# A hybrid HGRN2 and gMLP block on one core: blocks of w_out split at the border, and TensorE's work at the end of phase one held in written order

## The chip, the cores and the metric

The kernel runs on one core of a Trainium2 chip. A core has five engines with an instruction stream each: TensorE (PE in the profile, its weight loads PEld), VectorE (DVE), ScalarE (ACT), GpSimd (POOL) and SyncE (SP, which here issues the DMAs). Each works through its own stream in order; between engines, semaphores make an instruction wait for data or for a buffer. The metric is the device time of one execution in microseconds (us); lower is better.

## The reference

One layer of a diffusion backbone on 2048 latent tokens with a context prefix of 256 tokens, all in fp32:

```
h   = modulate(rmsnorm(x), shift1, scale1)             # 2048 x 1024
p   = h @ w_in                                         # 1024 -> 5*512 + 2*512 columns
o_f = gated recurrence, forward  (4 heads, 128x128 state, started from the context's state)
o_b = gated recurrence, backward (own forget gate)
o_hg  = rmsnorm(o_f + o_b) * silu(gate)                # per head of 128 channels
o_mlp = gelu(u) * (W_s layernorm(gelu(v)) + b)         # chunks of 128 positions
x   = x + g1 * (concat(o_hg, o_mlp) @ w_out)           # 1024 -> 1024
h2  = modulate(rmsnorm(x), shift2, scale2)
a,g = split(h2 @ w_up)                                 # 2 x 2816 columns
x   = x + g2 * ((a * gelu(depthwise_conv3x3(g) + b)) @ w_down)
out = rmsnorm(x, norm_final)
```

The six modulation vectors come from a product of silu(c) with w_ada.

## The kernel before

**Products.** An fp32 product is done as three passes on TensorE with operands split in two parts: hi is a rounded copy (a cast, by ScalarE, L133) and lo the rest (a subtraction, L134, by VectorE or GpSimd). The passes are hi·hi, hi·lo and lo·hi, so a 128-row block of the inner dimension takes three matmuls of 512 columns. Small products in the recurrence (banks named mi and sc) run on fp32 operands directly; one such 128x128 product is two records in the trace. All matmuls go through `T.matmul`, so their line is always L65, and all transposes are on L69.

**Phases.** Phase 1 (to 974 us) is the w_in projection, for the two halves of the tokens one after the other (hh = 0, 1) and in banks of 24 matmuls (`pj<-xh,whi`, `xl,whi`, `xh,wlo`). Phase 2 is the w_out product (`dn<-wo,o`, 16 tiles of 128 tokens, 48 matmuls each) with the second norm. Phase 3, to about 2007 us, is w_up, with a recursive scheme of fewer products (units ux and uz), and the convolution on VectorE and ScalarE (L1430, L1433). Phase 4 is w_down (`dn<-thl,mhl`), and then the rows' last norm and the stores.

**A head of the recurrence.** `hg` makes, for each head and half, the scores (sc), the products vt,kt that are the chunks' contributions to the states (`mi<-vt,kt`, copied to fs and bs_), and two chains over 8 chunks on VectorE (`chain`): the forward one over fs (L777), and the backward one over bs_ (L783). Then come the output products of a chunk, `mi<-vt,sc` (L895), `mi<-fs,Q` (L896) and in the second half of the tokens `mi<-bs_,Q` (L898). Four chunks make one tile on, which ScalarE copies out (L903) and squares for its norm (L758); GpSimd makes the root (rk, L128), VectorE scales by it (on<-on,rk, L737), TensorE transposes (`mi<-ident,on`), VectorE gates (L767), and a DMA stores the result to oT. The backward part of the first half has to wait for the second half's chain; `deferred` (L922) loads its data again (bs, Qb, op, sgb, L928 to L931), runs the backward chain and the products `mi<-bs,Qb` (L939), and goes the same way.

**Order.** All this is written as generators in two queues, hg_q and bg_q (class Pump). `yield w` means that the next step is due w us later on a clock that adds up estimated times of TensorE's matmuls (`T.t`). `slot()`, called between the matmuls of a projection bank, runs the steps that are due, and `later(fn, w)` adds a single step. So the steps of a head are mixed among pj matmuls. `drain()` runs all remaining steps at once and minds no due time. The instructions written in this way then go through a scheduler which may reorder them on each engine; `pin` (keep_in_program_order) holds an instruction at its written place among the pinned ones of its engine.

**The border from phase 1 to phase 2.** Ahead of the fourth last projection bank a hook calls `open_wo` (L1126):

```
hg_q.drain()
gates_done()
bg_q.drain()
```

Then it opens the pool for w_out's blocks and adds a step that loads the first o tile (L1138), the blocks wo (L1144) and, later, splits o tile 0. The blocks of w_out have been scaled by g1, split into hi and lo and stored to memory in the middle of phase 1 (`split` and `st` at L994 and L995). The raw data of o tile 1 are loaded at the start of phase 2 (L1316, `raw_o`). The last steps of the gMLP part, the products wsT,nt and the evictions nt (L717) with their stores (L686), stand at the very end of phase 1.

Of the kernel before, what the change touches and what calls it, by code (L numbers as in the profile page):

```python
# [32 lines left out]
LV = [1, 2, 4, 8, 16, 32, 64]  # L33
AL = 512


# [17 lines left out]
class Tensor:  # L54


    def __init__(self, engine):
        self.engine, self.t = engine, 0.0

    def matmul(self, out, lhsT, rhs, **kw):  # L60
        n = 1
        for _, count in rhs.ap[1:]:
            n *= count
        self.t += n / 2400 + 0.0135 if rhs.dtype == F32R else 2 * max(0.112, n / 1200 + 0.005)
        return self.engine.matmul(out, lhsT, rhs, **kw)  # L65

    def transpose(self, out, in_, identity):
        self.t += 0.109
        return self.engine.transpose(out, in_, identity)  # L69

# [13 lines left out]
def tile_trunk(ctx, tc, x, c, cx, c_ctx, w_ada, b_ada, norm_mix, norm_ffn, w_in, hg_norm, sgu_g, sgu_b,  # L84
# [14 lines left out]
    make_identity(nc, ident)  # L99
    ones = cst.tile([P, P], F32, name="ones")  # L100
    G.memset(ones, 1.0)
    ones_r = cst.tile([P, P], F32R, name="ones_r")
    nc.gpsimd.tensor_copy(ones_r, ones)
    vec = cst.tile([P, 50], F32, name="vec")
# [86 lines left out]
    with es1:  # L191
# [536 lines left out]
        def gate_later(hh, h, g0, on, r, sg):  # L728
            at = {"key": (hh, h), "to": (hh, h, g0, on, sg), "r": r}
            gates.append(at)  # L730
            hg_q.later(lambda: o_scale(at), 4.0)
            hg_q.later(lambda: gate_now(at), 7.5)

# [57 lines left out]
        def hg(hh, h, F, K, qs, vt, sgt):  # L791
# [90 lines left out]
            else:  # L882
# [3 lines left out]
                st(sg_d[h], sgt)  # L886
            yield 7.0 if hh == 1 else 4.0
            on = []
# [33 lines left out]
        def deferred(h):  # L922

            Qb = ph.tile([P, 2, TH], F32, tag="Q", name="Qb", align_bytes=AL)[:, 0, :]
            sgt = ph.tile([P, NCH + 1, P], F32, tag="fs", name="sgb")[:, :NCH, :].rearrange("p c t -> p (c t)")
            op = ph.tile([P, TH], F32, tag="S", name="op")
            bs_ = ph.tile([P, NCH + 1, P], F32, tag="bst", name="bs2")
            ld(bs_[:, :NCH, :], dh_d[h].rearrange("p (c t) -> p c t", t=P))  # L928
            ld(Qb, qb_d[h])
            ld(op, op_d[h])  # L930
            ld(sgt, sg_d[h])  # L931
            yield 5.0
            chain(bs_, True, hb[h], lambda i: tb0[h][:, i:i + 1])
            yield 4.0
            on = []
            for g in range(0, NCH, 4):
                po = bank("mi")
                for i in range(4):
                    T.matmul(po[:, i * P:(i + 1) * P], Qb[:, (g + i) * P:(g + i + 1) * P], bs_[:, g + i + 1, :],  # L939
                             start=True, stop=True)  # L940
# [41 lines left out]
        def w_out_ops():  # L982

            for n in range(2):
                cl = slice(n * 512, n * 512 + 512)
                g = pm.tile([P, 512], F32, tag="acc", name="g1")
                ld(g, g_d[0:1, cl].broadcast_to([P, 512]))
                for k in range(NK):
                    raw = raw_tile().rearrange("p (a c) -> p a c", a=2)
                    hi, w = raw[:, 0, :], raw[:, 1, :]  # L990
                    ld(w, w_out[k * P:(k + 1) * P, cl])
                    yield 8.0
                    V.tensor_mul(w, w, g)
                    split(hi.bitcast(F32R), w.bitcast(F32R), w, V)  # L994
                    st(wo_d[:, k, :, cl], raw)  # L995
                    yield 1.5
# [130 lines left out]
        def open_wo():  # L1127
# [8 lines left out]
            def load():  # L1136
                raw = raw_tile().rearrange("p (k c) -> p k c", c=P)
                ld(raw, oT_d[0][:, :, 0:P])  # L1138
                for k in range(early, NK):
                    wo.append(pw.tile([P, 2, D], F32R, name=f"wo{k}", align_bytes=AL))  # L1140
# [20 lines left out]
        bg_q.drain()  # L1161
        hg_q.flush()


# [14 lines left out]

    turn = [0]  # L1180

# [3 lines left out]
    def zbank():  # L1185
        return ps2.tile([P, 512], F32, tag="uz", name="uz", bufs=2)

# [4 lines left out]
    def dbank():  # L1192
        return ps2.tile([P, 2, 512], F32, tag="dn", name="dn", bufs=2)

    def a_tiles():
        return tuple(px.tile([P, 4, P], F32R, tag=w, name=w, bufs=4, align_bytes=AL) for w in ("Ah", "Al"))

# [3 lines left out]
    def c_tile():  # L1201
        return px.tile([P, NK, P], F32R, tag="fl", name="fl", bufs=2, align_bytes=AL)

# [4 lines left out]
    class Unit:  # L1208
# [15 lines left out]
        def prep(self, i):  # L1224
# [6 lines left out]
            if i == 1:  # L1231
                self.s2 = (c_tile()[:, :4, :].bitcast(F32) if self.slots[0] == 1 else
                           px.tile([P, 4, P], F32, tag="s1", name="s2"))
            split(hi, lo, (a11, a12, self.s2, a11, a21, a12, a22)[i])
# [38 lines left out]
    with tc.tile_pool(name="po", bufs=1, reuse_waits="tile") as po:  # L1273
        def second_norm(hh, g0, xs, ss, bank_, first, step):
# [6 lines left out]
            for k in range(4):  # L1281
# [14 lines left out]
                V.tensor_sub(fl[:, 6, :], fl[:, 1, :], fl[:, 2, :])  # L1296
                hi = px.tile([P, 7, P], F32R, tag="yst", name="yst", bufs=2, align_bytes=AL)
                a = b = 0
# [20 lines left out]
        def split_o(t, raw):  # L1319
            o = po.tile([P, 2, NK, P], F32R, tag="o", name="o", align_bytes=AL) if t % 2 else first_o[0]()  # L1320
            split(o[:, 0], o[:, 1], raw, V, pin)
# [6 lines left out]

        raw_o = {1: fetch_o(1)}
        xts = {0: fetch_x(0)}  # L1330
        ops = {0: first_o[1]}
        xs = []
# [208 lines left out]
    def cast(n, a, b, at, bt):  # L1541

        split(*at, a, V)
        split(*bt, b, V)
        ops[n] = *at, *bt
# [20 lines left out]
    for n, (u, i) in enumerate(prods):  # L1566
# [20 lines left out]
        if n == 12:  # L1587
            edges = px.tile([P, 7, P], F32R, tag="yst", name="edges", bufs=2, align_bytes=AL).bitcast(F32)
            edges = edges[:, :4, :].rearrange("p f (w c) -> p f w c", w=2)
# [129 lines left out]
    def root(ss, plus=D * EPS):  # L1719

        a, r = (pd_.tile([P, 1], F32, tag=t, name=t, bufs=4) for t in ("ra", "rr"))
        G.tensor_scalar(out=a, in0=ss, scalar1=plus, scalar2=None, op0=ALU.add)  # L1722
        G.tensor_tensor(out=r, in0=a, in1=mhalf[:, :1], op=ALU.pow)  # L1723
# [139 lines left out]
```

## Time and profile before

| | |
|---|---|
| median of 3 runs | 2437.95 us (2434.5 to 2441.58) |
| the profiled execution | 2440.39 us |
| its span, first to last instruction | 2438.6 us |
| mean granted clock of TensorE | 0.996 of full speed |
| TensorE busy | 2402.0 us, 99% |
| VectorE, ScalarE, GpSimd busy | 1656.9, 1043.2, 867.8 us |

The profiled execution is 2.44 us above the median and lies within the runs' scatter. In rows of the timeline the columns are the start, the length, the engine, the line and the operation, output<-inputs, the shape and how many instructions the row holds; in brackets stands how long the engine was idle before the row and what ended that. A row of several instructions runs from the first one's start to the last one's end, and matmuls overlap, so the spacing of many (11.15 us for 48) is the cost of one, not the length of a record. The granted clock is what the throttle allowed TensorE, 1.00 being full speed.

### The profile page before, as it was taken

The numbers are of one execution on the slowest core, as the hardware profiler recorded it, in microseconds if no ns is written. First come the engines' busy times: TensorE is split into PE (matmuls) and PEld (weight loads), VectorE is DVE, ScalarE is ACT, GpSimd is POOL, SyncE is SP. The second block draws the span as 40 slices with busy tenths as digits, with TensorE's granted clock in tenths as the row PEclk, the third lists the DMA queues.
The fourth block names the chain that finished last, engine by engine and source line by source line (L and its number), as shares of the span: only waits on it lengthen the run. The fifth ranks groups of instructions, "written<-read, shape, count | busy, mean of one in ns | idle before, by whom it ended". The sixth has DMA issues, their size and how long they took to land.

```text
span 2438.6 us, 32286 instructions
## 1 busy us (share of the span) xinstructions
PE 2402.0 (99%) x11711; PEld 1995.0 (82%) x11711; DVE 1656.9 (68%) x2253; ACT 1043.2 (43%) x1802; POOL 867.8 (36%) x788
## 2 busy tenths in 40 slices
PE   8999999999999999999999999999999999999998
PEld 5887887888888888788888888888888887888887
DVE  5757795765786785465596666639866772776875
ACT  3654344444444443354554444434445442332343
POOL 0021110210121122000688778787888870000002
PEclk9999999999999999999999999999999999999999
DMA  8365445463355234668922322562222238934755
GB/s 302 117 206 169 148 143 168 153 234 111 114 195 173 88 103 160 223 208 264 303 80 90 96 81 91 179 235 97 86 94 85 88 112 336 324 121 147 229 152 198
DMA packets 305581, 396.43 MB, mean 163 GB/s; under 512 B 32633, under 2 KB 215681, under 8 KB 302349
## 3 DMA queue, kind: packets, MB, share of 16 engines
q1 hardware_dynamic: 302132, 393.61, 48.6%
q8 instruction: 92, 1.51, 0.3%
q10 hardware_dynamic: 3289, 0.76, 0.1%
q14 instruction: 68, 0.56, 0.1%
HBM read 285.18 MB, written 109.13 MB: 162 GB/s over the span
## 4 chain that ended last, share of the span: by engine, by line
PE 54%; issue 2%; DMA 1%; DVE 1%; POOL 1%; ACT 1%; SPq 0%; POOLq 0%; ACTq 0%; DVEq 0%
PE dn L65 20%; PE ux L65 19%; PE uz L65 14%; PE pj L65 0%; POOL ra L1722 0%; DMA raw<-in_x_dram 0%; POOL rr L1723 0%; PE ux L69 0%; DMA raw<-in_w_up_dram 0%; DMA yf<-yd 0%; PE uz L69 0%; DVE dn L1433 0%; DMA yd<-fl 0%; POOL Al L134 0%; DVE cv L1357 0%
## 5 line engine op out<-in xcount | busy, mean ns | idle before, releaser
L1433 DVE SCALAR_TENSOR_TENSOR dn<-gp,taps,dn 128x1024 f32<-128x1024 f32 x352 | 448.2, 1284 | 97.5 <-ACT dn L1430 93.1
L65 PE MATMUL dn<-thl,mhl 128*128 128x512 f32 x1680 | 381.5, 389 | 1.2 <-ACT thl L133 1.2
L65 PEld LDWEIGHTS dn<-thl,mhl 128*128 128x128 f32 x1680 | 315.0, 188 | 67.7 <-ACT thl L133 2.1
L134 POOL TENSOR_TENSOR Al<-raw,Ah 128x512 fp32r<-128x512 f32 x264 | 341.7, 1311 | 65.8 <-ACT Ah L133 41.5
L65 PE MATMUL pj<-xh,whi 128*128 128x512 f32 x896 | 362.3, 405 | 0.3 <-ACT whi L133 0.3
L65 PE MATMUL pj<-xh,wlo 128*128 128x512 f32 x896 | 351.1, 392 | 1.2 <-DVE wlo L134 1.2
L65 PE MATMUL pj<-xl,whi 128*128 128x512 f32 x896 | 351.7, 393 | 0.0
L133 ACT CAST Ah<-raw 128x512 fp32r<-128x512 f32 x264 | 162.9, 620 | 238.9 <-PE ux L65 133.1
L65 PE MATMUL ux<-xah,Ah 128*128 128x512 f32 x528 | 205.7, 390 | 0.3 <-ACT keep L1497 0.3
L65 PEld LDWEIGHTS pj<-xh,wlo 128*128 128x128 f32 x896 | 168.3, 188 | 37.5 <-DVE wlo L134 2.1
L65 PEld LDWEIGHTS pj<-xh,whi 128*128 128x128 f32 x896 | 168.7, 188 | 34.2 <-issue 3.5
L65 PEld LDWEIGHTS pj<-xl,whi 128*128 128x128 f32 x896 | 168.9, 189 | 30.0 <-DVE xl L253 0.2
L65 PE MATMUL dn<-wo,o 128*128 128x512 f32 x768 | 184.4, 396 | 2.6 <-ACT o L133 2.1
L65 PE MATMUL uz<-yf,Ah 128*128 128x512 f32 x704 | 174.0, 389 | 0.0
L65 PEld LDWEIGHTS dn<-wo,o 128*128 128x128 f32 x768 | 143.0, 189 | 32.8 <-ACT o L133 2.5
L591 POOL TENSOR_TENSOR K<-K,tot 128x512 f32<-128x512 f32 x40 | 62.9, 1572 | 299.9 <-DVE tot L521 154.6
L65 PE MATMUL ux<-yf,Ah 128*128 128x512 f32 x528 | 155.4, 389 | 0.0
L65 PEld LDWEIGHTS uz<-yf,Ah 128*128 128x128 f32 x704 | 132.1, 188 | 27.4
L65 PE MATMUL ux<-xah,Al 128*128 128x512 f32 x528 | 141.8, 390 | 1.0 <-POOL Al L134 0.9
L65 PE MATMUL ux<-xal,Ah 128*128 128x512 f32 x352 | 137.0, 389 | 0.0
L1722 POOL TENSOR_SCALAR ra<-ss 128x1 f32<-128x1 f32 x8 | 5.3, 662 | 360.4 <-ACT jk L1714 360.4
L134 DVE TENSOR_TENSOR wlo<-raw,whi 128x1024 fp32r<-128x1024 f32 x68 | 84.1, 1236 | 68.3 <-ACT whi L133 67.3
(341 smaller groups left out, 4452.7 us busy)
## 6 DMA issues: line engine op xcount, KB each, us to landing
raw<-in_w_up_dram SPq DMA_DIRECT2D x88, 512.0 KB, 3.6
mr<-m SPq DMA_DIRECT2D x85, 512.0 KB, 5.5
raw<-in_w_in_dram SPq DMA_DIRECT2D x68, 512.0 KB, 4.0
sT<-wd SPq DMA_DIRECT2D x88, 256.0 KB, 5.8
raw<-in_w_ada_dram SPq DMA_DIRECT2D x32, 512.0 KB, 4.6
yf<-yd SPq DMA_DIRECT2D x14, 1024.0 KB, 10.4
m<-cv SPq DMA_DIRECT2D x22, 544.0 KB, 2.7
raw<-in_w_down_dram SPq DMA_DIRECT2D x22, 512.0 KB, 4.0
```

The lines of the kernel that those rows point to most:

```text
L65: return self.engine.matmul(out, lhsT, rhs, **kw)
L133: keep(S.copy(hi, raw))
L134: (eng or G).tensor_sub(lo, raw, hi.bitcast(F32))
L591: e.tensor_mul(view(K2, row * W + o, src), view(K, o, src), view(tot, t0, [[4, n], [ts, 2], [0, B]]))
L1433: V.scalar_tensor_tensor(out=cr, in0=gt[:, t // 3:t // 3 + RH, t % 3:t % 3 + GW], scalar=taps[:, t * NF + f:t * NF + f + 1], in1=cr, op0=A ...
L1722: G.tensor_scalar(out=a, in0=ss, scalar1=plus, scalar2=None, op0=ALU.add)
```

## The change

It has these parts; the prediction refers to them by number.

1. `LATE`: the w_out blocks 5, 6 and 7 are stored scaled but unsplit, loaded raw into the place of their lo part, and split after phase 1's last step, by six casts on ScalarE and six subtractions on VectorE, all pinned.
2. `T.keep`: class Tensor passes each instruction through a function that is the identity at first. In the last head, `hg` for (1, 3), it becomes `pin` once the states are written, and the identity again after phase 1's last step. In between all of TensorE's matmuls and transposes keep their written order.
3. Wider steps: the waits 7.5, 7.0 and 4.0 become 8.7, 8.5 and 4.8 for the last head's steps.
4. The raw data of o tile 1 are loaded in `open_wo`, into a tile of their own.
5. The tile ones goes; ones_r is made from ident, and the other users read it through a bitcast.
6. Pools of phases 2 and 3: the order of the first banks, one tag for Ah and Al with 8 buffers, two tags for uz, some alignments and a padded tile.
7. Phase 4: odd tiles 0 to 4 are allocated ahead of thl, and the evictions to odd (S.copy) and the casts of operands 3 and later are pinned.
8. The last norm's `root` adds a tensor operand with tensor_add in place of a tensor_scalar with a pointer.

```diff
+LATE = (5, 6, 7)
...
-        self.engine, self.t = engine, 0.0
+        self.engine, self.t, self.keep = engine, 0.0, lambda i: i
...
-        return self.engine.matmul(out, lhsT, rhs, **kw)
+        return self.keep(self.engine.matmul(out, lhsT, rhs, **kw))
...
-        return self.engine.transpose(out, in_, identity)
+        return self.keep(self.engine.transpose(out, in_, identity))
...
-    ones = cst.tile([P, P], F32, name="ones")
-    G.memset(ones, 1.0)
     ones_r = cst.tile([P, P], F32R, name="ones_r")
-    nc.gpsimd.tensor_copy(ones_r, ones)
+    nc.gpsimd.tensor_scalar(out=ones_r, in0=ident, scalar1=0.0, scalar2=1.0, op0=ALU.mult, op1=ALU.add)
+    ones = ones_r.bitcast(F32)
...
-            hg_q.later(lambda: gate_now(at), 7.5)
+            hg_q.later(lambda: gate_now(at), 8.7 if (hh, h) == (0, NH - 1) else 7.5)
...
-            yield 7.0 if hh == 1 else 4.0
+            if (hh, h) == (1, NH - 1):
+                T.keep = pin
+            yield 8.5 if (hh, h) == (1, NH - 1) else 7.0 if hh == 1 else 4.0
...
             chain(bs_, True, hb[h], lambda i: tb0[h][:, i:i + 1])
-            yield 4.0
+            yield 4.8 if h == NH - 1 else 4.0
...
-                    split(hi.bitcast(F32R), w.bitcast(F32R), w, V)
-                    st(wo_d[:, k, :, cl], raw)
+                    if k in LATE:
+                        st(wo_d[:, k, 0, cl], w)
+                    else:
+                        split(hi.bitcast(F32R), w.bitcast(F32R), w, V)
+                        st(wo_d[:, k, :, cl], raw)
...
-                        ld(wo[k][:, :, sl].bitcast(F32), wo_d[:, k, :, sl])
+                        if k in LATE:
+                            ld(wo[k][:, 1, sl].bitcast(F32), wo_d[:, k, 0, sl])
+                        else:
+                            ld(wo[k][:, :, sl].bitcast(F32), wo_d[:, k, :, sl])
+                raw1 = pw.tile([P, NK, P], F32, name="raw1")
+                ld(raw1, oT_d[0][:, :, P:2 * P])
+                first_o.append(raw1)
                 yield 17.0
...
         hg_q.flush()
+        T.keep = lambda i: i
+        for n in range(2):
+            sl = slice(n * 512, n * 512 + 512)
+            for k in LATE:
+                t = wo[k][:, :, sl]
+                split(t[:, 0], t[:, 1], t[:, 1].bitcast(F32), V, pin)
...
-        raw_o = {1: fetch_o(1)}
+        raw_o = {1: first_o[1]}
...
-        split(*at, a, V)
-        split(*bt, b, V)
+        keep = pin if 3 <= n < 6 * NJ else lambda i: i
+        split(*at, a, V, keep)
+        split(*bt, b, V, keep)
...
+    odd = [pd_.tile([P, 2, 512], F32, name=f"odd{i}") for i in range(5)]
     thl = pd_.tile([P, 3, 2, 512], F32R, name="thl", align_bytes=AL)
-    odd = [pd_.tile([P, 2, 512], F32, name=f"odd{i}") for i in range(NCH)]
+    odd += [pd_.tile([P, 2, 512], F32, name=f"odd{i}") for i in range(5, NCH)]
...
-        G.tensor_scalar(out=a, in0=ss, scalar1=plus, scalar2=None, op0=ALU.add)
+        if isinstance(plus, float):
+            G.tensor_scalar(out=a, in0=ss, scalar1=plus, scalar2=None, op0=ALU.add)
+        else:
+            G.tensor_add(a, ss, plus)
...
-            S.copy(o[:, q // 2, :], pd)
+            pin(S.copy(o[:, q // 2, :], pd))
```

What this does to the order of instructions is seen on TensorE at the end of phase 1. Before, the first outputs of the last head stand among projection matmuls; here is TensorE's order from the last states (vt,kt) on:

```order
L65 MATMUL mi<-vt,kt 128x128 x16
...
L65 MATMUL mi<-vt,sc 128x128
L65 MATMUL mi<-fs,Q 128x128
...
L65 MATMUL pj<-xh,whi 128x512
L65 MATMUL pj<-xl,whi 128x512
L65 MATMUL pj<-xh,wlo 128x512
...
L65 MATMUL mi<-bs__7975,Q 128x128
```

From vt,kt to the last transposes of on stand 55 pj matmuls in all, and 41 come behind those. A bit later in the same stream, still before the change, are the products of `deferred` (bs, Qb) and the transposes of on:

```order
L65 MATMUL pj<-xh,whi 128x512
L65 MATMUL pj<-xl,whi 128x512
L65 MATMUL mi<-bs_8079,Qb 128x128 x4
L69 MATMUL mi<-ident,on 128x128 x8
L65 MATMUL pj<-xh,wlo 128x512
L65 MATMUL pj<-xh,whi 128x512
L65 MATMUL mi<-bs_8079,Qb 128x128 x4
L65 MATMUL pj<-xl,whi 128x512
```

Here too pj matmuls stand ahead of the first four products, behind the first eight transposes and behind the second four products. After the change, TensorE has from the same states on:

```order
L66 MATMUL mi<-vt,kt 128x128 x16
L66 MATMUL mi<-vt,sc 128x128
L66 MATMUL mi<-fs,Q 128x128
L66 MATMUL mi<-bs__7961,Q 128x128
...
L66 MATMUL mi<-bs_8065,Qb 128x128 x4
L70 MATMUL mi<-ident,on 128x128 x8
L66 MATMUL mi<-bs_8065,Qb 128x128 x4
L70 MATMUL mi<-ident,on 128x128 x8
L66 MATMUL pj<-xh,whi 128x512
L66 MATMUL pj<-xl,whi 128x512
L66 MATMUL pj<-xh,wlo 128x512
```

No pj matmul is left between the states and the last transposes, and all 96 follow them; the lines of the new file are one higher here. The rows left out hold the other outputs of the head, three products a chunk.

SyncE's queue at the border was, before the change:

```order
L1144 DMA wo_8181<-wo_d 128x2x512
L1144 DMA wo_8182<-wo_d 128x2x512
L1144 DMA wo_8183<-wo_d 128x2x512
L686 DMA oT_80<-nt 128x512 x2
L1316 DMA raw<-oT_79 128x8x128
L1326 DMA raw<-in_x_dram 128x1024
L1316 DMA raw<-oT_79 128x8x128
```

The load of o tile 1's raw data, the first raw<-oT here, stands behind both stores of nt. After the change the queue is:

```order
L1150 DMA wo<-wo_d 128x512 x3
L1152 DMA wo<-wo_d 128x2x512 x2
L1150 DMA wo<-wo_d 128x512 x3
L1154 DMA raw_8180<-oT_77 128x8x128
L686 DMA oT_78<-nt 128x512 x2
L1347 DMA raw<-in_x_dram 128x1024
L1337 DMA raw<-oT_77 128x8x128
```

The load of o tile 1's raw data (raw_8180) has moved ahead of the two stores of nt, and six of the wo loads carry half the data.

More of the change, by code (lines that the diff above doesn't have):

```diff
@@ L1139, in load @@
                 for k in range(early, NK):
-                    wo.append(pw.tile([P, 2, D], F32R, name=f"wo{k}", align_bytes=AL))
+                    wo.append(pw.tile([P, 2, D], F32R, tag="wo", name="wo", bufs=NK - early, align_bytes=AL))
                 for n in range(2):
@@ L1178, in tile_trunk @@
     xal = pb.tile([P, NR - 1, 4, 512], F32R, tag="xal", name="xal", align_bytes=AL)
-    turn = [0]
+    turn = [0, 0]
     def xbank():
@@ L1185, in zbank @@
     def zbank():
-        return ps2.tile([P, 512], F32, tag="uz", name="uz", bufs=2)
+        turn[1] += 1
+        return ps2.tile([P, 512], F32, tag=f"uz{turn[1] % 2}", name="uz")
     def ubank():
@@ L1193, in dbank @@
         return ps2.tile([P, 2, 512], F32, tag="dn", name="dn", bufs=2)
+    for first in (xbank, zbank, dbank, zbank):
+        first()
     def a_tiles():
-        return tuple(px.tile([P, 4, P], F32R, tag=w, name=w, bufs=4, align_bytes=AL) for w in ("Ah", "Al"))
+        return tuple(px.tile([P, 4, P], F32R, tag="A", name=w, bufs=8, align_bytes=AL) for w in ("Ah", "Al"))
     def v_tile():
@@ L1201, in c_tile @@
     def c_tile():
-        return px.tile([P, NK, P], F32R, tag="fl", name="fl", bufs=2, align_bytes=AL)
+        return px.tile([P, NK, P], F32R, tag="fl", name="fl", bufs=2)
     def raw_tile2(j):
@@ L1232, in prep @@
                 self.s2 = (c_tile()[:, :4, :].bitcast(F32) if self.slots[0] == 1 else
-                           px.tile([P, 4, P], F32, tag="s1", name="s2"))
+                           px.tile([P, 4 * P + 80], F32, tag="s1", name="s2")[:, :4 * P].rearrange("p (k c) -> p k c", k=4))
             split(hi, lo, (a11, a12, self.s2, a11, a21, a12, a22)[i])
@@ L1296, in second_norm @@
                 V.tensor_sub(fl[:, 6, :], fl[:, 1, :], fl[:, 2, :])
-                hi = px.tile([P, 7, P], F32R, tag="yst", name="yst", bufs=2, align_bytes=AL)
+                hi = px.tile([P, 7, P], F32R, tag="yst", name="yst", bufs=2)
                 a = b = 0
@@ L1319, in split_o @@
         def split_o(t, raw):
-            o = po.tile([P, 2, NK, P], F32R, tag="o", name="o", align_bytes=AL) if t % 2 else first_o[0]()
+            o = po.tile([P, 2, NK, P], F32R, tag="o", name="o") if t % 2 else first_o[0]()
             split(o[:, 0], o[:, 1], raw, V, pin)
@@ L1327, in fetch_x @@
             return xt.rearrange("p a b -> p (a b)")
-        raw_o = {1: fetch_o(1)}
+        raw_o = {1: first_o[1]}
         xts = {0: fetch_x(0)}
-        ops = {0: first_o[1]}
+        ops = {0: first_o[2]}
         xs = []
@@ L1587, in tile_trunk @@
         if n == 12:
-            edges = px.tile([P, 7, P], F32R, tag="yst", name="edges", bufs=2, align_bytes=AL).bitcast(F32)
+            edges = px.tile([P, 7, P], F32R, tag="yst", name="edges", bufs=2).bitcast(F32)
             edges = edges[:, :4, :].rearrange("p f (w c) -> p f w c", w=2)
```

## The prediction

> **What bounds the kernel now.** I read the busy times of the page first, then its chain of what ended last:
>
> ```profile
> PE 2402.0 (99%) x11711; PEld 1995.0 (82%) x11711; DVE 1656.9 (68%) x2253; ACT 1043.2 (43%) x1802; POOL 867.8 (36%) x788
> PE 54%; issue 2%; DMA 1%; DVE 1%; POOL 1%; ACT 1%; SPq 0%; POOLq 0%; ACTq 0%; DVEq 0%
> ```
>
> TensorE is busy in nearly the whole span of 2438.6 us. So an edit counts if it opens or closes idle time on TensorE, or changes its clock. What can be closed is in TensorE's list of waits:
>
> ```profile
> PE dn L65 <- ACT o L133: 2.1, 1, 2.1
> PE dn L65 <- DVE o L134: 0.5, 1, 0.5
> PE dn L65 <- ACT thl L133: 1.2, 2, 0.8
> PE mi L65 <- DVE bs__7975 L783: 0.6, 1, 0.6
> ```
>
> Columns: total, count, longest. The first two are the stall on o tile 1, the third is phase 4, and the last is the place that edit 2 touches. The timeline shows that place and the border to the w_out product; in 128x128 fp32 rows two records are one product:
>
> ```profile
> 935.64 0.39 PE L65 MATMUL mi<-vt,sc 128*128 128x128 f32 x2
> 936.84 0.49 PE L65 MATMUL mi<-fs,Q 128*128 128x128 f32 x2 [0.37 <-DVE fs L777]
> 939.34 0.46 PE L65 MATMUL mi<-bs__7975,Q 128*128 128x128 f32 x2 [0.63 <-DVE bs__7975 L783]
> 943.80 0.39 PE L65 MATMUL mi<-bs__7975,Q 128*128 128x128 f32 x2
> 951.95 1.13 PE L65 MATMUL mi<-bs,Qb 128*128 128x128 f32 x8 [0.47 <-issue]
> 959.27 0.63 PE L69 MATMUL mi<-ident,on 128*128 128x128 f32 x4 [1.00 <-DVE on L737]
> 961.04 0.65 PE L69 MATMUL mi<-ident,on 128*128 128x128 f32 x4 [0.45 <-DVE on L737]
> 973.57 11.15 PE L65 MATMUL dn<-wo,o 128*128 128x512 f32 x48
> 986.80 0.73 PE L65 MATMUL dn<-wo,o 128*128 128x512 f32 x2 [2.08 <-ACT o L133]
> 988.06 18.24 PE L65 MATMUL dn<-wo,o 128*128 128x512 f32 x73 [0.52 <-DVE o L134]
> ```
>
> Between 936 and 962 TensorE idles only 0.37 + 0.63 + 0.47 + 1.00 + 0.45 = 2.9 us, because projection products (pj) fill the time that VectorE, ScalarE and POOL need for the head's chain of steps.
>
> **Edit 2 and 3, the written order and the wider steps.** In the order of before, 55 pj products stand between the last state product (vt,kt) and the last transposes of on; 41 follow. In the order of after none stands between and all 96 follow: the drain at the border runs the rest of the head at one go, so the wider waits (8.5, 8.7, 4.8) have nothing to act on, and I cost edit 3 at 0. The other engines' orders there are unchanged. So TensorE meets three waits bare. Their ends come from these rows of VectorE, ScalarE and SyncE:
>
> ```profile
> 938.46 2.28 DVE L783 SCALAR_TENSOR_TENSOR bs__7975<-bs__7975,tot 128x128 f32<-128x128 f32 x6
> 945.14 0.56 ACT L903 COPY on<-mi 128x512 f32<-128x512 f32 x1
> 948.56 0.69 DVE L737 TENSOR_TENSOR on<-on,rk 128x512 f32<-128x512 f32 x1 [1.23 <-POOL rk L128]
> 949.17 2.67 DVE L783 SCALAR_TENSOR_TENSOR bs<-bs,tb 128x128 f32<-128x128 f32 x7
> 944.27 0.32 SPq L928 DMA_DIRECT2D bs<-dh  x1
> ```
>
> A: the third product of the written order (bs,Q of chunk 0) needs the last of the backward chain's steps, which end at 938.46 + 2.28 = 940.74. vt,sc and fs,Q of chunk 0 are through at about 936.1 (935.64 and two products). Idle 4.7 us.
> The 22 products left take 22 x 0.23 = 5.1 us (943.80 - 939.34 = 4.46 for about 20), so they end at 945.9, 1.7 later than before (943.80 + 0.39 = 944.2).
> B: now the second half is copied out by ScalarE, normed, scaled (on<-on,rk), and then comes VectorE's second backward chain. Before, the copy began at 945.14, behind the first half's squares, and the chain at 949.17. Now it can begin at about 945.95, 0.8 later, while the reload of the states (bs<-dh), which waits for TensorE's last read, goes out 1.7 later. The chain slips by 0.8 to 1.7; I take 1.0, near the lower end, since the scaling at 948.56 and not the load was last before. The first bs,Qb product comes at about 952.95: idle 7 us.
> C: the gaps from that product to the two transposes of on are the same work, 959.27 - 951.95 = 7.32 and 961.04 - 959.27 = 1.77, so they begin at 960.3 and 962.0, with some 4.0 and 1.3 us idle in front.
> Up to here the head is 1.0 late. But the 55 products still have to be done: 55 x 11.15/48 = 12.7, with the 0.2275 us spacing inside such a run 12.5. Slip at full clock: 12.5 + 1.0 = **+13.5**.
>
> **What the idle time does to the clock.** The windows of 1 us around the stall on o tile 1 (busy time, granted clock, DMA share, GB/s):
>
> ```profile
> 985.00:986.00 1.00, 0.00 (x0) 1.00 1.14 332
> 986.00:987.00 1.00, 0.20 (x1) 1.00 0.84 306
> 987.00:988.00 1.00, 0.53 (x2) 0.81 0.23 84
> 988.00:989.00 1.00, 0.94 (x2) 0.50 0.07 29
> 990.00:991.00 1.00, 1.00 (x4) 0.50 0.68 178
> 991.00:992.00 1.00, 1.00 (x5) 0.98 1.14 382
> 956.00:962.00 6.00, 4.55 (x26) 1.00 0.09 35
> ```
>
> After 2.08 + 0.52 us idle the granted clock was 0.50 from about 987.6 to 991.0, 3.4 us in which half the work was done: 1.7 us lost. The 1.00 + 0.45 us at 957 to 961 cost no clock. A, B and C are each longer than 2.6 us. A dip behind A or C falls on dense products, 1.7 each; behind B only about 2.7 us of products stand before C's wait, so at most 1.1 reaches the path: 1.7 + 1.1 + 1.7 = **+4.5**. Ends: 0 and, with a fourth, 6.8.
> The Trainium skill (TensorE: Matmul & The Clock Gate, Part 1) says that the clock is halved after at least one wholly idle window of about 3.4 us. The trace disagrees: it fell after 2.08 and 0.52 us with work in between. By that rule the sum would hold 1.7 for one dip, behind B, in place of 4.5.
>
> **Edit 4, o tile 1's raw data loaded ahead of the stores.** What held it before, and the late split's neighbours:
>
> ```profile
> 973.43 2.95 SPq L686 DMA_DIRECT2D oT<-nt  x2
> 976.48 0.83 SPq L1316 DMA_DIRECT2D raw<-oT  x1
> 973.85 0.75 DVE L717 SCALAR_TENSOR_TENSOR nt<-mi,vec,rh 128x512 f32<-128x512 f32 x1 [1.59 <-PE mi L65]
> L134 DVE TENSOR_TENSOR raw<-raw x16: 673/688/1767, 376.7 to 537.5; 128x512 fp32r<-128x512 f32 x16
> ```
>
> The load went out at 976.48, behind two stores that waited for the last nt. Moved ahead of them it depends only on the o stores of phase 1's first half, which stand earlier in SyncE's queue; the two stores now stand behind it and keep their own wait for the last nt. The 2.08 + 0.52 and the dip go: **-2.6 - 1.7 = -4.3**.
>
> **Edit 1, three w_out blocks split at the border.** Six casts and six of the 16 subtractions of the last row (its figures: least, median, most ns) leave the time from 376 to 537 us. No wait of TensorE there that I found ends on them: 0. They come back behind the last nt, which VectorE ends at 974.60, 1.03 after the product's start. At 0.69 each, block 5's first half is ready 1.7 after that start; its products are the 16th and later, due at 15 x 0.2275 = 3.4. The others follow with more room, and o tile 1 is due only after 11.15. Cost 0, with a cover of 1.7; if all six had to be through first, 6 x 0.69 + 1.03 - 3.4 = 1.8, with a dip 3.5. The loads are half as large; nothing waits for them.
>
> **Edits 5 to 8.** Rows for phase 4, the tail and the start:
>
> ```profile
> 2027.75 12.58 PE L65 MATMUL dn<-thl,mhl 128*128 128x512 f32 x54 [0.75 <-ACT thl L133]
> 2072.07 8.25 PE L65 MATMUL dn<-thl,mhl 128*128 128x512 f32 x35 [0.46 <-ACT thl L133]
> 2433.04 0.50 POOL L1722 TENSOR_SCALAR ra<-oss 128x1 f32<-128x1 f32 x1 [1.56 <-ACT dn L1748]
> 14.89 0.19 POOL L126 TENSOR_SCALAR rs<-xss 128x2 f32<-128x2 f32 x1 [12.31 <-ACT xjk L239]
> 1.45 4.42 PE L65 MATMUL pj<-ident 128*128 128x128 f32 x24 [1.45 <-POOL ident masks.py:199]
> 1.63 0.95 POOL L269 MEMSET acc<- 128x1024 f32 x1
> 6.98 3.59 PE L65 MATMUL pj<-wa,cs 128*2 128x512 f32 x8 [1.10 <-DMA wa<-in_w_ada_dram]
> ```
>
> Casts of thl no longer stand behind evictions (pinned in written order): at best both waits go, -1.2; at worst 0, as the pins only reorder ScalarE. I take **-1.2**. The last root's add gets a tensor operand in place of a pointer: 0.50 could fall to the 0.19 of an add with constants, or stay; **-0.3**, of the 0.0 to -0.3 that one link of the tail allows. At the start ident comes some 0.85 later, behind the 0.95 memset and with the one of ones gone: the 4.42 us of warming products end at 6.7 in place of 5.9, and the first real ones wait for data until 6.98: 0, with 0.3 of cover. Pools and paddings of phases 2 and 3 move no instruction: 0.
>
> **Sum.** 13.5 + 4.5 - 4.3 - 1.2 - 0.3 = +12.2 us, against the profiled execution (2440.39 us, 2.4 above the median). On the median of 2437.95 that gives **2450 us**.
>
> **Rivals.**
> The clock falls only when TensorE idles through one whole stretch of 3.4 us, the length of the dip at 987.6. Such stretches laid end to end, only B's 7 us is certain to hold one: 13.5 + 1.7 - 5.8 = +9.4, 2447.3 us. Against it stands that this dip came without such a stretch. Chance 0.12. This is the rule of the Trainium skill named above (TensorE: Matmul & The Clock Gate, Part 1).
> No clock loss at all, as at 957 to 961: 13.5 - 5.8 = +7.7, 2445.6. These stretches are three times as long. 0.07.
> The other side: the border is covered. If TensorE's waits A to C held projection products after all, since the steps are due later, the slip would be 0 and the gains alone remain, -5.8: 2432 us. It decides once the slip falls under 5.8, which needs 34 of the 55 products back between the waits. The row at 951.95 speaks for such a cover before; the new order, where none stands, against. 0.10.
> The late split stalls the w_out product: 1.8 plus a dip of 1.7 on top of the sum, 2453.5. 0.10.
>
> **How the numbers follow.** The forecast as summed has 0.61, its own range 2447 to 2453 (clock 1.7 to 6.8, chain 0.8 to 1.7). The range given, 2444 to 2456, takes in the two clock rivals with the scatter of the runs, and at the top the late split with a fourth dip; it leaves out the covered border. 0.3% is 7.3 us, about what a measurement of this kernel can tell from no change: under 2430.6 is faster (half of the covered border and a little more, 0.06), up to 2445.3 the same (the other half, half of the case without clock loss, a tail of the forecast, 0.12), the rest slower, 0.82.
>
> **What would show it.** Right: bs,Q of chunk 0 near 940.8 behind 4 to 5 us of idle that ends on the chain of L783; the first bs,Qb near 953 behind 6 to 7 us; transposes near 960 and 962; 96 pj products behind them; 1-us windows at clock 0.50 between 940 and 966; the first w_out product near 991.6; no wait on o tile 1; no waits on thl. Wrong: pj products between these steps, a clock of 1.00 throughout, a wait at wo blocks 5 to 7, or the w_out product starting before 980.

## The result, and the profile after

| | before | after |
|---|---|---|
| median of 6 runs | 2436.95 us (2434.5 to 2441.58) | 2452.74 us (2449.3 to 2455.43) |
| ratio of the times | | 1.0061, 95% interval 1.0051 to 1.0071 |
| the profiled execution | 2440.39 us | 2452.68 us |
| its span | 2438.6 us | 2450.9 us |

The changed kernel is slower by 0.6%, some 15 us by the ratio. On another chip, beside 18 runs of the kernel before (median 2439.93), it took 2452.25 us, a ratio of 1.0052 (1.0040 to 1.0065). The two profiled executions differ by 12.3 us; they are what the terms below are read from.

TensorE's list of waits in the changed kernel begins with three that were not there:

```profile
PE mi L66 <- DVE bs L783: 7.3, 1, 7.3
PE mi L66 <- DVE bs__7961 L783: 4.6, 1, 4.6
PE mi L70 <- DVE on L737: 4.4, 2, 3.8
```

The waits on o (2.1 and 0.5) and on thl (1.2) are gone from the list. The timeline of TensorE at the border shows where the three lie:

```profile
936.06 0.39 PE L66 MATMUL mi<-vt,sc 128*128 128x128 f32 x2
936.28 0.39 PE L66 MATMUL mi<-fs,Q 128*128 128x128 f32 x2
941.31 0.74 PE L66 MATMUL mi<-bs__7961,Q 128*128 128x128 f32 x2 [4.64 <-DVE bs__7961 L783]
...
947.70 0.39 PE L66 MATMUL mi<-bs__7961,Q 128*128 128x128 f32 x2
955.42 2.05 PE L66 MATMUL mi<-bs,Qb 128*128 128x128 f32 x8 [7.33 <-DVE bs L783]
...
964.07 1.09 PE L70 MATMUL mi<-ident,on 128*128 128x128 f32 x4 [3.75 <-DVE on L737]
965.85 1.11 PE L70 MATMUL mi<-ident,on 128*128 128x128 f32 x4 [0.69 <-DVE on L737]
966.62 0.78 PE L66 MATMUL pj<-xh,whi 128*128 128x512 f32 x1
...
992.16 28.15 PE L66 MATMUL dn<-wo,o 128*128 128x512 f32 x123
1020.16 0.79 PE L70 MATMUL ux<-ident,cv 128*128 128x128 f32 x4
```

The third output product waits 4.64 us for the last step of the backward chain, the first bs,Qb 7.33, the transposes 3.75 and 0.69; all projection products follow. The clock fell in each of the long waits or right at its end (windows of 1 us; busy time, granted clock, DMA share, GB/s):

```profile
940.00:941.00 1.00, 0.00 (x0) 1.00 0.55 229
942.00:943.00 1.00, 1.00 (x7) 0.50 0.00 0
945.00:946.00 1.00, 1.00 (x11) 1.00 0.00 0
...
952.00:953.00 1.00, 0.00 (x0) 0.50 0.99 406
957.00:958.00 1.00, 1.00 (x7) 0.50 0.00 0
959.00:960.00 1.00, 0.83 (x7) 1.00 0.04 14
...
963.00:964.00 1.00, 0.00 (x0) 0.50 0.00 0
967.00:968.00 1.00, 1.00 (x3) 0.50 0.63 240
969.00:970.00 1.00, 1.00 (x6) 1.00 1.16 301
```

Seven records stand in a window at 0.50, eleven at 1.00. Place by place, each kernel against its own rows:

| place in TensorE's stream | before | after | difference |
|---|---|---|---|
| first vt,sc of the last head | 935.64 | 936.06 | +0.42 |
| first w_out product | 973.57 | 992.16 | +18.59 |
| the first ux<-ident,cv behind o tile 1 | 1006.14 | 1020.16 | +14.02 |
| the products of phase 4 where the first wait on thl was | 2027.75 | 2041.09 | +13.34 |
| end of the span | 2438.6 | 2450.9 | +12.3 |

So the border costs 18.17 us, o tile 1 gives back 4.57, and all that follows, phase 4 and the tail among it, 1.72. The first rows of the table of before stand in the prediction; these two belong to it (before, then after):

```profile
1006.14 0.73 PE L69 MATMUL ux<-ident,cv 128*128 128x128 f32 x4
```

```profile
2041.09 1.30 PE L66 MATMUL dn<-thl,mhl 128*128 128x512 f32 x5
```

### The profile page after: what moved, and what is told of

It is laid out like the page before. It is cut to its first block, busy times and chain, and to the rows that moved or that the text cites. A ratio compares the mean times of both kernels' runs of the same rounds, so it can differ in the third digit from the quotient of the medians.

```text
span 2450.9 us, 32290 instructions
## 1 busy us (share of the span) xinstructions
PE 2404.2 (98%) x11711; PEld 1999.0 (82%) x11711; DVE 1657.2 (68%) x2253; ACT 1043.8 (43%) x1802; POOL 866.2 (35%) x787
## 4 chain that ended last, share of the span: by engine, by line
PE 47%; issue 2%; POOL 1%; ACT 0%; DVE 0%; DMA 0%; POOLq 0%; SPq 0%; ACTq 0%
PE ux L66 19%; PE dn L66 14%; PE uz L66 14%; POOL rr L1749 0%; DMA raw<-in_w_up_dram 0%; POOL Al L134 0%; POOL ra L1748 0%; POOL ra L1746 0%; ACT jk L1737 0%; POOL raw L1263 0%; DVE odd L81 0%; DVE dn L1454 0%; POOL raw L1261 0%; POOL s L1259 0%; POOL fl L1259 0%
```

## The experiments

All ratios are against the kernel before on the same chip. A number that serves throughout is the length of the border, from the first vt,sc of the last head to the first w_out product in the profiled execution: 37.93 us before, 56.10 after.

### The pinned order taken out

```diff
-            if (hh, h) == (1, NH - 1):
-                T.keep = pin
```

> The changed kernel without part 2: T.keep stays the identity, all else stays. TensorE's order at the end of phase 1 is then that of the kernel before, with 55 projection matmuls between the last states and the last transposes. Theory (the pinned order leaves three waits bare and lets the clock fall): the 18.2 us by which the w_out product began later in the changed kernel's trace (992.16 against 973.57, less 0.42 that was there before the last head) go, and the gains of the other parts stay: 2452.7 - 18.2 = 2434.5, and by the sum of the prediction 2437 - 5.8 = 2431; so 2431 to 2434.5, with the three long waits under 1 us each. Rival (the late split, the loads or the pools make the slip): about 2450 and the waits on the backward chain stay at 4 to 7 us.

Measured: 2434.64 us, ratio 0.9977 (0.9969 to 0.9986), so 5.6 us faster than the kernel before. The border is back at 37.93 us, and none of the three long waits is left:

```profile
933.15 0.39 PE L66 MATMUL mi<-vt,sc 128*128 128x128 f32 x2
...
971.08 28.15 PE L66 MATMUL dn<-wo,o 128*128 128x512 f32 x123
```

The slip hangs on the pinned order, and the late split costs the w_out product nothing: its 123 products run through. With 2440.01 for the kernel before on this chip, the sum of the prediction (less 5.8) is met. So this version beats both kernels.

What part 3 does is seen in the next run, which has the pinned order and the old waits of 7.5, 7.0 and 4.0. In its trace TensorE's instructions stand in the same order from 700 us to the w_out product as in the changed kernel's, so the wider steps move nothing there.

### The pinned order alone

```diff
+        self.engine, self.t, self.keep = engine, 0.0, lambda i: i
...
+            if (hh, h) == (1, NH - 1):
+                T.keep = pin
             yield 7.0 if hh == 1 else 4.0
...
         hg_q.flush()
+        T.keep = lambda i: i
```

> The kernel before with part 2 alone: the pinned order, old waits of 7.0, 7.5 and 4.0 us, no late split, o tile 1 loaded as before. Theory: the whole slip of 18 us, 2437 + 18 = 2455, and with the stall on o tile 1 still there (2 to 3 us of wait on its cast). Rival (the pinned order costs only its idle time, not the clock): 2437 + 13.5 = 2450.5. Rival (the slip needs the other parts): near 2437.

Measured: 2457.72 us, ratio 1.0070 (1.0058 to 1.0082), 17.1 us slower. The border took 58.04 us, 20.1 more than before. The half clock held on longer than in the changed kernel: behind the first wait from 941.4 to 948.2, two stretches of 3.4 us in place of one.

```profile
942.00:943.00 1.00, 0.55 (x2) 0.50 0.00 0
947.00:948.00 1.00, 1.00 (x7) 0.50 0.00 0
949.00:950.00 1.00, 1.00 (x12) 1.00 0.00 0
```

One part of the expectation was wrong: there was no stall on o tile 1, though nothing was changed there. SyncE's and ScalarE's rows show it:

```profile
971.01 0.54 SPq L1146 DMA_DIRECT2D wo<-wo_d  x1
973.34 6.96 SPq L1146 DMA_DIRECT2D wo<-wo_d  x9
998.15 0.56 SPq L1319 DMA_DIRECT2D raw<-oT  x1
```

```profile
1003.15 1.05 ACT L133 CAST o<-raw 128x1024 fp32r<-128x1024 f32 x1 [7.92 <-DMA raw<-in_x_dram]
```

The load of o tile 1 still stands behind the two stores and goes out 2.9 us after the w_out product's start (995.25), as before. Yet the cast begins 7.9 us after that start, where it was 12.1 before. What differs is that nine of the ten loads of w_out go out 22 us ahead of the product instead of 9. That pointed away from part 4. In this row and in those of the same cast below, the profile names the load of x (raw<-in_x_dram), issued next behind that of o tile 1, as what ended the wait. By the semaphore updates in the traces it can't have been: the load of x landed 1.1 to 1.2 us after the cast had begun, in this kernel at 1004.34.

### Part 4 taken out, part 1 taken out, both, and part 1 alone

These are four kernels without the pinned order. The first is the kernel of the first experiment with o tile 1 loaded at the start of phase 2 again:

```diff
-                raw1 = pw.tile([P, NK, P], F32, name="raw1")
-                ld(raw1, oT_d[0][:, :, P:2 * P])
-                first_o.append(raw1)
...
-        raw_o = {1: first_o[1]}
+        raw_o = {1: fetch_o(1)}
...
-        ops = {0: first_o[2]}
+        ops = {0: first_o[1]}
```

> The first of these kernels (no pinned order) without part 4 too: o tile 1's raw data are loaded at the start of phase 2 again, behind the two stores of nt. Theory: the stall on o tile 1 comes back, 2.6 us of idle time and 1.7 us of half clock, so 4.3 us above the first kernel. Rival (the late split delays the casts, so the stall is longer than before): 6 us or more. Rival (the gain at o tile 1 came from elsewhere): no difference.

Measured: ratio 0.9973 (0.9964 to 0.9982), the same as with part 4 (0.9977), and no stall: the second rival, the gain came from elsewhere. The next leaves part 4 in and takes part 1 out:

```diff
-LATE = (5, 6, 7)
+LATE = ()
```

> The first kernel (no pinned order) without part 1: all blocks of w_out split in the middle of phase 1 and loaded in full, ten loads of 512 KB at the border in place of four of 512 and six of 256; o tile 1 is still loaded ahead of the two stores. Theory A (o tile 1 was late because its load was issued behind the stores): no stall, same time as the first kernel. Theory B (it was late because 5.1 MB of w_out had to pass the DMA queues first): 1.5 MB more at about 400 GB/s is 3.8 us later data; the load goes out right behind them, at about 972, so it would be there at about 980 and the cast still in time: no stall either, but the cast about 3 us later than in the first kernel. If the stall comes back in full (2.6 us of wait, 4.3 us in all), the place of the load in the queue does nothing.

Measured: ratio 0.9993 (0.9984 to 1.0002), 0.16% above the kernel with part 1, and the stall is back, if shorter than before. Both theories had expected none:

```profile
968.76 0.57 SPq L1152 DMA_DIRECT2D raw<-oT  x1
```

```profile
981.05 1.04 ACT L133 CAST o<-raw 128x1024 fp32r<-128x1024 f32 x1 [11.33 <-DMA raw<-in_x_dram]
```

```profile
969.74 11.15 PE L66 MATMUL dn<-wo,o 128*128 128x512 f32 x48
982.14 0.73 PE L66 MATMUL dn<-wo,o 128*128 128x512 f32 x2 [1.26 <-ACT o L133]
983.40 8.91 PE L66 MATMUL dn<-wo,o 128*128 128x512 f32 x38 [0.53 <-DVE o L134]
```

The load went out ahead of the stores, 1.0 us before the w_out product, and the cast began 12.3 us later all the same. The load is not the whole of that: by the semaphore updates it had landed at 979.61, 10.85 us after its issue, and the second store of nt at 980.87, 0.18 us before the cast. Both edits of the last two kernels together:

> The first kernel (no pinned order) without parts 1 and 4 both. The kernel without part 4 alone had no stall at o tile 1, so part 4 by itself isn't the reason that it is gone. Theory B (the bytes at the border): with both taken out the stall is back, 2 to 3 us of wait on o's cast with a dip of the clock behind, 4.3 us above the first kernel. Rival (another part, such as the pools of phase 2, took the stall away): no stall, same time as the first kernel.

Measured: ratio 0.9995 (0.9986 to 1.0004); the stall is back with 1.82 and 0.53 us. And the other way round, the kernel before with nothing but part 1 (the hunks of part 1 in the change):

> The kernel before with part 1 alone: blocks 5 to 7 of w_out stored and loaded raw and split at the border; o tile 1 is still loaded behind the two stores, TensorE's order isn't pinned. Theory (the bytes at the border made o tile 1 late): the loads are 1.5 MB less, 3.8 us at 400 GB/s, so its cast begins about 8.6 us after the w_out product's start in place of 12.1, the wait of 2.1 + 0.5 us and the dip behind it go: 4.3 us less, ratio 0.9982. Rival (it takes the early load too): the stall stays, ratio 1.

Measured: ratio 0.9985 (0.9976 to 0.9994), 3.7 us faster, and no wait on o:

```profile
972.86 17.50 PE L66 MATMUL dn<-wo,o 128*128 128x512 f32 x76
```

```profile
976.09 0.59 SPq L1328 DMA_DIRECT2D raw<-oT  x1
```

```profile
981.44 1.05 ACT L134 CAST o<-raw 128x1024 fp32r<-128x1024 f32 x1 [3.45 <-DMA raw<-in_x_dram]
```

When the cast of o tile 1 begins, counted from the first w_out product; it has to begin by about 11.15 - 1.05 - 1.22 = 8.9 us if TensorE isn't to wait (its own length, and that of the subtraction behind it):

| | wo loads in full | part 1: six of ten at half size |
|---|---|---|
| loaded behind the stores | 12.1 before, 11.9 without parts 1, 2 and 4 | 8.6 in both kernels |
| loaded ahead (part 4) | 11.3 | 7.3 |

Part 1 moves the cast by 3.3 to 4.0 us, part 4 by 0.6 to 1.3. Single executions of the same code differ too: in the kernel of the last experiment below, which has this border unchanged, the cast began after 11.4 us and not 12.1. So the effect of part 4 with full loads, 0.6 to 0.8, can't be told from that scatter; that of part 1 can.

Why part 4 does so little is seen in what landed last. The times are from the semaphore updates in the traces, in us from the first w_out product:

| kernel | second store of nt landed | load of o tile 1 landed | cast began |
|---|---|---|---|
| before | 10.2 | 12.0 | 12.1 |
| without parts 1, 2 and 4 | 10.0 | 11.7 | 11.9 |
| part 4 without part 1 | 11.1 | 9.9 | 11.3 |
| part 1 without part 4 | 5.9 | 8.5 | 8.6 |
| parts 1 and 4, no pin | 7.1 | 5.8 | 7.3 |
| changed kernel | 5.0 | 7.2 before the product | 5.2 |

The cast begins 0.2 us behind the later of the two. Part 4 brings the data 1.8 to 2.6 us earlier, and then the cast waits for the store. In the changed kernel, where the data had been there for 12 us, the profile names the store itself:

```profile
997.33 1.05 ACT L133 CAST o<-raw 128x1024 fp32r<-128x1024 f32 x1 [2.07 <-DMA oT<-nt]
```

Why the cast has to wait for the stores no run shows; that the second buffer of o lies where the tiles nt were is a guess.

The table of DMA issues between 962 and 985 us in the kernel before gives the loads' sizes and the median time to landing; below it a window of TensorE's view with DMA share and GB/s:

```profile
wo<-wo_d SPq DMA_DIRECT2D x10, 512.0 KB, 10.6
raw<-oT SPq DMA_DIRECT2D x3, 512.0 KB, 7.8
```

```profile
974.00:984.00 10.00, 10.00 (x46) 1.00 1.06 396
```

The queues were full, at 396 GB/s, in the ten microseconds before the stall; 1.5 MB less is 3.9 us at that rate, about what part 1 gained. With fewer bytes ahead of them the stores land earlier as well as the load (5.9 and 7.1 us in the table, where it was 10.0 and 11.1). The Trainium skill (DMA: Bandwidth & Descriptors, Queues, rings and completion order) says that each DMA engine takes the descriptors of a queue in the order of its ring; from that it would follow that a late load waits for the bytes ahead of it, and the traces agree: a load put right behind the ten full loads, ahead of the stores, took 10.85 us to land, and 4.82 in the kernel with the pin alone, where nine of them had gone out 25 us before it.

### Idle products in the waits

keep_busy(n, "sc") issues n products of ident with itself into a bank that nobody reads; its own lines are left out here.

```diff
...
+                    if (hh, h, ch) == (1, NH - 1, 0):
+                        keep_busy(18, "sc")
                     if hh == 1:
                         T.matmul(o, Q[:, 0, sl], bs_[:, ch + 1, :], start=False, stop=True)
...
+                if h == NH - 1 and g == 0:
+                    keep_busy(28, "sc")
...
+                if h == NH - 1 and g == 4:
+                    keep_busy(14, "sc")
```

> The changed kernel with 60 small products of ident with itself, into a bank that nobody reads, put into the three waits: 18 ahead of the first bs,Q, 28 ahead of the first bs,Qb and 14 ahead of the last transposes, at 0.2225 us each a little less than the idle time there, so that they hold the clock up and delay nothing. Theory (the half clock behind each wait costs time on the path, 1.6 + 1.3 + 1.4 by the spacing of the products in the changed kernel's trace): 4.3 us faster than the changed kernel, about 2448.4, and no 1-us window at 0.50 between 936 and 970. Rival (only the dense projection products behind the last wait matter, the chains of VectorE set the rest): 1.4 us faster. Rival (the clock is not the matter): the same time.

Measured: ratio 1.0040 (1.0028 to 1.0052). The border took 53.36 us, 2.7 less than in the changed kernel. Two dips are gone and the third stayed, behind the last transposes, where TensorE had still been idle for half of the time; the row of this stretch, and the dip behind it:

```profile
960.50:963.90 3.40, 1.62 (x13) 0.99 0.00 0
```

```profile
964.00:967.00 3.00, 3.00 (x9) 0.50 0.40 141
```

So a second filling, 16 products there and 4 between the two groups of transposes:

> The kernel with idle products in the waits again, with 16 in place of 14 ahead of the first of the last transposes and 4 more between these two, where the clock had still fallen. Theory (the clock falls when TensorE was busy for less than about half of some 3.4 us): no window at 0.50 from 936 to 975, and 1.4 us more off than with the first filling, 4.3 us below the changed kernel in all. Rival (it falls here for another reason): a dip again behind the last transposes.

Measured: ratio 1.0031 (1.0019 to 1.0043), and the changed kernel beside it, run again, 1.0052:

> The changed kernel itself once more, beside the two others on one chip: ratio 1.006 as before, three dips of the clock between 940 and 970, of 1 or 2 times 3.4 us each.

The clock stayed at 1.00 through the whole border in the filled kernel; the same stretch of the changed kernel's second profile stands below:

```profile
934.00:975.00 41.00, 38.05 (x280) 1.00 0.53 181
```

```profile
934.00:975.00 41.00, 24.31 (x121) 0.79 0.49 168
```

The border took 52.27 us with the filling and 56.18 without: the half clock costs 3.9 us, and the rest of the slip, 52.27 - 37.93 = 14.3, is there at full clock. By the medians of that chip the difference is 2452.25 - 2448.30 = 4.0.

### The border two banks later

```diff
-        i = len(seq) - 4
+        i = len(seq) - 2
```

> The changed kernel with its border (the drain and what follows) two banks later, 48 projection matmuls on; the pinned order stays. TensorE then has 42 projection matmuls between the last states and the first outputs, and 48 behind the last transposes. Theory (each bare wait costs its idle time and its dip): the first wait (4.6 us and 1.6 us of half clock) is covered, the other two stay, so 6.2 us faster than the changed kernel, about +9 us against the kernel before; the loads of w_out come later relative to its product, with up to 4 us of stall as the upper end. Rival (any pinned order costs about as much): +15 us as the changed kernel.

Measured: 2452.19 us, ratio 1.0047 (1.0035 to 1.0060). The first wait was covered, as expected (vt,sc comes at 944.41 behind projection products and waits for nothing), the second and third were not (7.6 and 3.8), and the w_out product stalled at its first tile:

```profile
985.29 0.73 PE L66 MATMUL dn<-wo,o 128*128 128x512 f32 x2 [1.62 <-ACT o L133]
986.79 23.42 PE L66 MATMUL dn<-wo,o 128*128 128x512 f32 x102 [0.77 <-DVE o L134]
```

From the first vt,kt to the first w_out product it is 54.44 us, against 59.67 in the changed kernel (932.49 to 992.16): 5.2 less, with the stall's 1.62 inside it. By the ratios (1.0047 against 1.0061 and 1.0052) the whole gain is 1 to 3 us, which is within the scatter. That one covered wait saves time agrees with the theory; its 6.2 us is not settled by this run.

### Part 7 alone

```diff
-        split(*at, a, V)
-        split(*bt, b, V)
+        keep = pin if 3 <= n < 6 * NJ else lambda i: i
+        split(*at, a, V, keep)
+        split(*bt, b, V, keep)
...
+    odd = [pd_.tile([P, 2, 512], F32, name=f"odd{i}") for i in range(5)]
     thl = pd_.tile([P, 3, 2, 512], F32R, name="thl", align_bytes=AL)
...
-            S.copy(o[:, q // 2, :], pd)
+            pin(S.copy(o[:, q // 2, :], pd))
```

> The kernel before with part 7 alone (odd tiles 0 to 4 allocated ahead of thl, the casts and the evictions to odd pinned). Theory: both waits on the casts of thl (0.75 at 2027.75, 0.46 at 2072.07 in the kernel before) go and nothing else moves: 1.2 to 1.7 us less, about 0.06%, which shows in the trace and hardly in the times. Rival (the waits went in the changed kernel because its phase 4 began later or with other buffers): both waits stay.

Measured: ratio 0.9997 (0.9989 to 1.0006), which is no difference that these runs can tell. In the trace both waits on thl are gone, with a gain of under 2 us. The theory holds for the waits; what they are worth is read from the trace alone.

The border is that of the kernel before, so this trace also shows how far the stall on o tile 1 varies between executions:

```profile
984.09 0.73 PE L65 MATMUL dn<-wo,o 128*128 128x512 f32 x2 [1.34 <-ACT o L133]
```

With the 0.53 us behind it that is 1.87 us of idle time, and the clock stayed at 1.00, where the kernel before had 2.60 and a time of half clock.

## Why the prediction was right

The forecast was 2450 us, the changed kernel took 2452.74, inside the forecast's own range of 2447 to 2453 too. Against the profiled execution it said +12.2 us, and the profiled executions differ by 12.3. By its steps:

**The bare waits (A, B, C).** Predicted idle 4.7, 7, 4.0 and 1.3 us; found 4.64, 7.33, 3.75 and 0.69. The places forecast for the steps (953, 960 and 962) left the half clock out; they came at 955.42, 964.07 and 965.85. The slip at full clock was said to be 13.5; the filled kernel shows 14.3. The difference lies in B. I took the chain's slip as 1.0, since the scaling and not the reload had been last. In the changed kernel the reload was last:

```profile
948.17 0.32 SPq L930 DMA_DIRECT2D bs<-dh  x1
```

```profile
952.64 2.67 DVE L783 SCALAR_TENSOR_TENSOR bs<-bs,tb 128x128 f32<-128x128 f32 x7 [0.39 <-DMA bs<-dh]
```

The chain waited 0.39 us for the data, and 0.80 us in the filled kernel, so the upper end, 1.7, was the right one: in the filled kernel the first bs,Qb comes 18.15 us after the first vt,sc (935.25 to 953.40), where it was 16.31 before, 1.8 later.

**The clock.** Three dips, as forecast, one behind each wait. The term of +4.5 measured 3.8 to 3.9 in the changed kernel (56.10 and 56.18, each less 52.27). Against the filled kernel the first bs,Qb is 1.2 us later, the stretch from there to the last transposes 1.3 longer and the rest 1.3, where the prediction had 1.7, 1.1 and 1.7. It varies from run to run: in the kernel with the pin alone it was 58.04 - 52.27 = 5.8. The slip at full clock was set 0.8 too low and the clock 0.7 too high; that the two cancelled in the sum for the border, 18.0 against 18.17, is luck.

**O tile 1.** The size fits (-4.3, measured -4.57), the step was wrong. It said that the load was late because two stores stood ahead of it, gave the whole gain to part 4, and said of part 1's smaller loads that "nothing waits for them". The runs show that part 4 alone leaves a stall, that part 1 alone removes it, and that the pinned order alone removes it too, by giving the loads 13 us more. Two things were missed. The transfers had the w_out blocks' bytes ahead of them; the issue at 976.48, which I read, tells when a transfer was handed over and not when it could run, and the row with a DMA share of 1.14 at 985 us, which stood in the prediction for the sake of the clock, was the one to read. And the cast waits for the stores of nt too, so a load moved ahead of them gains little. That the size fits is in part luck: it takes in a time of half clock which the kernel before had in its profiled execution, and which was missing behind the 1.87 us of the same stall in the kernel with part 7 alone.

**The other edits.** Part 1's late split cost TensorE nothing, and the wider waits left TensorE's order at the border as it was, as said. Phase 4 and the tail were forecast at -1.5; all that follows o tile 1 gave -1.72; the tail's add takes 0.41 us now, not the 0.19 that its own term reached for:

```profile
2442.73 0.41 POOL L1748 TENSOR_TENSOR ra<-oss 128x1 f32<-128x1 f32 x1 [1.67 <-ACT dn L1774]
```

Ident came later by 0.8 and the first real products by 0.2 (7.16 against 6.98), inside the +0.42 that the last head starts later by.

**The rivals.** The clock dipped three times and not once, so the rule that it falls only after one whole idle stretch is out here: the third dip came after a stretch with 1.61 of 3.41 us busy (958.42 to 961.83, shown in the last section). That is the rule of the Trainium skill (TensorE: Matmul & The Clock Gate, Part 1), and the trace disagrees with it. The covered border is what the kernel without the pin shows, and 5.6 us faster against the 5.8 worked out for it. It wasn't this kernel, since its written order has nothing to cover with.

## What to carry to other kernels

Holding an engine to its written order is only as good as that order: a drain that runs all remaining steps at once writes a chain of other engines' work with nothing between, and a scheduler that is free to move independent products there was worth 18 us. Price such a wait twice, once for the idle time and once for the half clock behind it. And where a tile comes late, read the busy share of the DMA engines and the bytes queued ahead of it before its place in the issuing queue, and look for everything that its consumer waits for, not its load alone.

## What the runs showed of the hardware

The granted clock fell to 0.50 although TensorE had not been idle throughout. In one trace the falls lie a whole number of 3.41 us apart: 941.35, 951.59 and 961.83 in the changed kernel, three steps each. Cut into such stretches between 920 and 1000 us, the thirteen traces show 14 that end in a fall, and TensorE was busy in them for 0 up to 1.64 of 3.41 us. In every other stretch at full clock it was busy for 1.79 us or more. So the bound lies between 1.64 and 1.79 of 3.41 us, near half. The rows are the third dip of the changed kernel, the highest with a fall (the first filling) and the lowest without one (the border two banks later):

```profile
958.42:961.83 3.41, 1.61 (x12) 1.00 0.41 154
```

```profile
960.43:963.85 3.42, 1.64 (x14) 1.00 0.00 0
```

```profile
982.03:985.44 3.41, 1.79 (x9) 1.00 1.08 370
```

Each time of half clock there lasted about 3.4 us or twice that (941.4 to 944.8, 951.6 to 958.4, 961.8 to 968.7 in the changed kernel). It went on for a second stretch where TensorE had been busy for at most 2.34 us of the first (the pin alone, 941.38 to 944.79), and ended where it had been busy for 2.80 or more. So the place of a wait among these stretches bears on whether it costs a dip, and how long a one. Whether that is why single runs of these kernels scatter by some 3 us was not tested.
